# Half of the tokens take most of an input projection by Strassen's seven block products

## The chip, the cores and the metric

The kernel runs on one core of a Trainium2 chip. The core has five engines that each work through their own list of instructions in order: TensorE (PE, with a separate row PEld for its weight loads), VectorE (DVE), ScalarE (ACT), GpSimd (POOL) and SyncE (SP), which here only issues DMAs. An engine waits on semaphores for what the others produce. The metric is device time in microseconds (us) of one execution, as the median of several runs.

## The reference, cut to what matters

One layer over 2048 tokens of width 1024, in float32:

```python
h = _rmsnorm(x, norm_g[l])
proj = h @ w_in[l] + b_in[l]                       # 1024 -> 4096
ua, za, ub, zb, ga, gb = jnp.split(proj, SPLITS, axis=-1)
ya = _s5_branch(ua, ...) * jax.nn.silu(za)         # diagonal complex state-space scan, gelu, glu
yb = _pool_branch(ub, pool_w[l], pool_scale[l]) * jax.nn.silu(zb)   # causal means over 2, 4, 8, 16
merged = sigmoid(ga) * (ya @ w_branch_a[l]) + sigmoid(gb) * (yb @ w_branch_b[l])
x = x + merged @ w_out[l]
return _rmsnorm(x, final_norm_g)
```

The parts ua, za, ub and zb are 512 columns wide (4 tiles of 128 each, called UA, ZA, UB, ZB with a number), ga and gb 1024 (8 tiles each, GA and GB).

## The kernel before, in words

Tokens lie in four chunks of 512. Every product is done in three: each operand is cut into a high and a low part (`split`, L94: ACT writes the high part, DVE or POOL subtracts to get the low part), and `mm3` (L103 to L106) adds high*high, high*low and low*high in PSUM. A tile of 128 columns for one chunk is one block (`proj_block`, L594): 8 steps over the 1024 inputs, 24 matmuls of 128x512. The transposed, normalised input of a chunk, `hT`, is held in SBUF from its making to the end of the projection, all four chunks side by side.

The order of work is written out by hand; each engine does its share of it in the order of the text.

1. The ua part goes chunk by chunk. While a chunk's four blocks run, the next chunk is squared and summed on ACT (L544), scaled by POOL (L554), transposed on TensorE and cut (`transpose_tile`, L560). Chunk 3, say, is scaled beginning at the last block of chunk 1 and transposed behind the third block of chunk 2.
2. The za part: 4 tiles over 4 chunks, each block ending in `silu2` (L843: two passes of ACT from PSUM, one of DVE). After each block one step of the generator `matrices` is issued; its steps hold work on POOL (`outputs`, L477 to L479), DVE (`inputs`) and TensorE (L504, L507).
3. The ub and zb parts with the pooled means (`slide`, L877, L878 and L880; then L920) on DVE, cut by `cut_pooled`, multiplied on TensorE and scaled by `mix`. The cut of the means of one window is issued among the ub blocks of the next.
4. The ga and gb parts, 64 blocks. Each ends in one pass of ACT from PSUM (L1029) and a DMA. After each block one step of the generator `scan` is issued. A group u of it has 7 steps: `run_scan` (L749 to L766, all DVE), `table` (DVE), `run_taps` (TensorE), cuts, and last `run_out`, `run_in` and `gelu`, which run straight into the next `run_scan`: TensorE's small products (psy, psx), eight copies and a square on ACT, a pass of POOL (L784), two passes of DVE from PSUM (L787), a tanh, two more of DVE (L790). `phases` comes once, ahead of the first table.
5. The glu, branch and output products.

The projection's results lie in the PSUM pool `pmm`, four banks taken in turn (`mmtile`, L69); TensorE can begin a block only when the reader of the block four before it is done. Weights come from SP's DMAs one tile ahead (`pump`, L133).

## Time and profile before

| | us |
|---|---|
| median of 3 runs (lowest, highest) | 1214.21 (1213.85, 1217.29) |
| the profiled execution's own time | 1216.58 |
| its span | 1214.7 |
| TensorE busy | 1180.5 (97%) |
| VectorE busy | 731.5 (60%) |
| ScalarE busy | 395.0 (33%) |
| GpSimd busy | 345.9 (28%) |

The span is the time from the first to the last instruction that the profiler saw; the execution's own time is a little longer. Busy times of engines that are not awaited cost nothing. A matmul's row has a duration, but matmuls overlap: the distance between the starts of two of them is what one costs. TensorE's granted clock is given as a share of full speed: 1.00 is 2.4 GHz, and a stretch that reads less had some of its time at 1.2 GHz. In a timeline the number in brackets is the engine's idle time ahead of the instruction and who ended it.

### The profile page before, as it was taken

To read this page: it belongs to the slowest core of one execution; us is meant where nothing else is said; L and a number is where in the kernel's file an instruction comes from. 1 tells how busy PE (TensorE), PEld (TensorE's weight loads), DVE (VectorE), ACT (ScalarE), POOL (GpSimd) and SP (SyncE) were. 2 spreads that over 40 slices of the span, in tenths; PEclk is the share of its full clock that TensorE was granted. 3 is DMA by queue.
4 is the path that set the end of the run, shared out by engine and by line. 5 is a ranking of instruction groups with operands and counts; after the bars stand their busy time and mean duration, and the time that the engine had idled before them with its cause. 6 is when DMAs were issued, how large, how long until landed. Compare 5 with 4: busy or idle time off the path is not lost. (4 is left out here: it accounts for less than half of the span.)

```text
span 1214.7 us, 14777 instructions
## 1 busy us (share of the span) xinstructions
PE 1180.5 (97%) x5413; PEld 976.0 (80%) x5413; DVE 731.5 (60%) x1310; ACT 395.0 (33%) x622; POOL 345.9 (28%) x232
## 2 busy tenths in 40 slices
PE   7999989999999999999999999998999999999996
PEld 5887867888888888888888888886888888888885
DVE  5586389153543668777798773045665855755715
ACT  6542212222222232443333432244333332322302
POOL 3321077111111222422334321223562312213312
PEclk9999999999999999999999999999999999999998
DMA  8412334201111232433334332177766564563503
GB/s 297 139 44 77 67 108 135 81 18 55 44 46 44 86 111 88 132 96 109 113 95 131 98 101 81 69 233 241 255 217 224 172 196 136 182 212 109 191 1 104
DMA packets 149783, 149.94 MB, mean 123 GB/s; under 512 B 23584, under 2 KB 111184, under 8 KB 149712
## 3 DMA queue, kind: packets, MB, share of 16 engines
q1 hardware_dynamic: 127424, 112.28, 30.7%
q10 hardware_dynamic: 22288, 36.73, 8.0%
q8 instruction: 42, 0.69, 0.2%
q14 instruction: 29, 0.24, 0.1%
HBM read 99.43 MB, written 49.55 MB: 123 GB/s over the span
## 5 line engine op out<-in xcount | busy, mean ns | idle before, releaser
L104 PE MATMUL mm<-hT,wt 128*128 128x512 f32 x960 | 377.2, 393 | 0.0
L105 PE MATMUL mm<-hT,wt 128*128 128x512 f32 x960 | 375.6, 391 | 0.2 <-DVE hT L100 0.2
L106 PE MATMUL mm<-hT,wt 128*128 128x512 f32 x960 | 374.9, 390 | 0.0
L105 PEld LDWEIGHTS mm<-hT,wt 128*128 128x128 f32 x960 | 181.1, 189 | 38.0 <-DVE hT L100 1.3
L106 PEld LDWEIGHTS mm<-hT,wt 128*128 128x128 f32 x960 | 180.9, 188 | 38.0
L104 PEld LDWEIGHTS mm<-hT,wt 128*128 128x128 f32 x960 | 181.3, 189 | 36.8
L98 POOL TENSOR_TENSOR wt<-raw,wt 128x1024 fp32r<-128x1024 f32 x30 | 85.9, 2862 | 306.9 <-ACT wt L96 306.9
L1029 ACT ACTIVATE go<-mm,half 128x512 f32<-128x512 f32 x64 | 43.9, 687 | 192.5 <-PE mm L106 192.1
L104 PE MATMUL mm<-yab,wt 128*128 128x512 f32 x256 | 99.9, 390 | 0.1
L105 PE MATMUL mm<-yab,wt 128*128 128x512 f32 x256 | 99.7, 389 | 0.0
L106 PE MATMUL mm<-yab,wt 128*128 128x512 f32 x256 | 99.7, 389 | 0.0
L96 ACT ACTIVATE wt<-raw 128x1024 fp32r<-128x1024 f32 x62 | 65.5, 1057 | 57.2 <-PE mm L106 29.3
L1123 POOL TENSOR_TENSOR r<-r,gb 128x512 f32<-128x512 f32 (+1 forms) x33 | 40.9, 1257 | 135.3 <-ACT xt L1120 135.3
L1165 POOL TENSOR_TENSOR m<-gt 128x512 f32<-128x512 f32 x32 | 52.2, 1630 | 95.7 <-DVE gt L1163 64.5
L98 DVE TENSOR_TENSOR wt<-raw,wt 128x1024 fp32r<-128x1024 f32 x32 | 59.9, 1871 | 18.1 <-ACT wt L96 18.0
L847 ACT ACTIVATE st<-mm,half 128x512 f32<-128x512 f32 x32 | 22.0, 688 | 141.0 <-PE mm L106 104.8
L1163 DVE SCALAR_TENSOR_TENSOR gt<-gt,mm 128x512 f32<-128x512 f32 x64 | 42.3, 680 | 28.8 <-PE mm L106 24.3
L104 PEld LDWEIGHTS mm<-yab,wt 128*128 128x128 f32 x256 | 48.1, 188 | 10.9 <-issue 0.5
L106 PEld LDWEIGHTS mm<-yab,wt 128*128 128x128 f32 x256 | 48.1, 188 | 10.0
L105 PEld LDWEIGHTS mm<-yab,wt 128*128 128x128 f32 x256 | 48.1, 188 | 9.8
L105 PE MATMUL mm<-wo,mt 128*128 128x512 f32 (+1 forms) x136 | 51.2, 377 | 0.0
L106 PE MATMUL mm<-wo,mt 128*128 128x512 f32 (+1 forms) x136 | 51.2, 377 | 0.0
(272 smaller groups left out, 1918.2 us busy)
## 6 DMA issues: line engine op xcount, KB each, us to landing
xt<-in_x SPq DMA_DIRECT2D x32, 512.0 KB, 4.8
raw<-in_w_in SPq DMA_DIRECT2D x32, 512.0 KB, 4.2
Gd<-go ACTq DMA_DIRECT2D x64, 256.0 KB, 2.2
gt<-Gd SPq DMA_DIRECT2D x32, 512.0 KB, 4.9
raw<-in_w_branch_a SPq DMA_DIRECT2D x32, 256.0 KB, 2.8
raw<-in_w_branch_b SPq DMA_DIRECT2D x32, 256.0 KB, 3.2
out<-r ACTq DMA_DIRECT2D x32, 256.0 KB, 2.3
Ud<-uo ACTq DMA_DIRECT2D x16, 256.0 KB, 2.1
```

The source lines that it names most:

```text
L96: A.activation(hi, src, AF.Copy, scale=1.0 if scale is None else scale)
L98: (eng or V).tensor_tensor(out=lo, in0=src, in1=hi.bitcast(F32), op=ALU.subtract)
L104: PE.matmul(ps, lhsT=sh, rhs=mh, start=first, stop=False)
L105: PE.matmul(ps, lhsT=sh, rhs=ml, start=False, stop=False)
L106: PE.matmul(ps, lhsT=sl, rhs=mh, start=False, stop=last)
L847: A.activation(t, ps, AF.Tanh, bias=hcol(n), scale=0.5)
L1029: A.activation(o, ps, AF.Tanh, bias=hcol(n), scale=0.5)
L1123: GP.tensor_tensor(out=r, in0=r, in1=gb[:, cs], op=ALU.mult)
L1163: V.scalar_tensor_tensor(out=gt[:, b], in0=gt[:, b], scalar=1.0, in1=pss[b], op0=ALU.add, op1=ALU.mult)
L1165: GP.tensor_tensor(out=m, in0=gt[:, 0], in1=gt[:, 1], op=ALU.add)
```

## The change

The chunks are taken in the order 2, 3, 0, 1 (`CH`). For chunks 0 and 1 everything but the ua part is computed by Strassen's method in Winograd's form: a pair of column tiles, two chunks and two halves of the 1024 inputs make a 2x2 block product, and seven products of half-length blocks take the place of eight. There are 14 pairs. One run of seven is a `unit`.

- Seven slots of SBUF (`SLOTS`) hold the input's blocks B11, B21, B22 and their sums T1 to T4. `sums` and `last_sum` make them in the ua part of chunks 0 and 1. Chunks 2 and 3 use the same slots first; their transposed input is written to DRAM (`Hd`) and read back (`back`) in the last unit.
- `s_make` makes a pair's seven weight operands, among them four sums, three products ahead. Weight tiles other than ua's are loaded twice, 60 loads in place of 32; the pools `raw` and `w` have 3 buffers in place of 2.
- `unit` runs the seven products of 12 matmuls each. The first result is copied out of PSUM by ACT; the others are added by DVE (`plus`), and `sink` does what the tile's kind asks for. Results of ub and zb go by way of DRAM (`UBd`, `ZBd`).
- `matrices` is stepped in units 1 to 5, at every second product (`beside(0.5)`); `scan`, now with 6 steps a group, from unit 6 on at 0.36 of a step per product, then at 1.0 per za block, 0.4 per block of the ub, zb and ga parts, and 1.0 per gb block.
- Chunks 2 and 3 follow with ordinary blocks: za, then for each window two ub blocks, two zb blocks and four ga blocks, with the cuts and `mix` of that window's means among the ga blocks; then gb.

```diff
@@ -46,8 +46,8 @@
-    rawp = ctx.enter_context(tc.tile_pool(name="raw", bufs=2))
-    wp = ctx.enter_context(tc.tile_pool(name="w", bufs=2))
+    rawp = ctx.enter_context(tc.tile_pool(name="raw", bufs=3))
+    wp = ctx.enter_context(tc.tile_pool(name="w", bufs=3))
@@ -62,6 +62,9 @@
+    UBd = [dram.tile([128, 2, 512], F32, name=f"UBd{n}") for n in range(NB)]
+    ZBd = [dram.tile([128, 2, 512], F32, name=f"ZBd{n}") for n in range(NB)]
+    Hd = {c: [dram.tile([128, 2, 512], F32R, name=f"Hd{c}_{k}") for k in range(NK)] for c in (2, 3)}
...
@@ -172,14 +172,17 @@
+    CH = (2, 3, 0, 1)
+    SLOTS = ("B11", "T2", "B21", "T1", "T3", "B22", "T4")
+    s_slot = {name: ExitStack() for name in SLOTS}
+    slot = {name: sub(s_slot[name], "p" + name, "right").tile([128, 2, NB, 512], F32R, name=name) for name in SLOTS}
+    blocks = {2: ("T2", "T4"), 3: ("T3", "B22"), 0: ("B11", "B21"), 1: ("T3", "B22")}
+
+    def part(c, p, k):
+        return slot[blocks[c][k // NB]][:, p, k % NB, :]
...
@@ -561,42 +556,173 @@
+    def first_blocks(k):
+
+        wholes[k] = t = rawp.tile([128, 1024], F32, tag="raw", name="b11")
+        whole(t[:, 0:512], "B11", k, GP)
+        whole(t[:, 512:1024], "B21", k, GP)
+
+    def sums(k):
+
+        ps = [transpose_tile(1, k), transpose_tile(1, k + NB)]
+        t = wholes.pop(k)
+        t1, t4 = t[:, 0:512], t[:, 512:1024]
+        t2 = stg.tile([128, 512], F32, tag="stg", name="t2")
+        V.scalar_tensor_tensor(out=t1, in0=ps[0], scalar=gcol(k), in1=t1, op0=ALU.mult, op1=ALU.subtract)
+        V.scalar_tensor_tensor(out=t2, in0=ps[1], scalar=gcol(k + NB), in1=t1, op0=ALU.mult, op1=ALU.subtract)
+        V.tensor_tensor(out=t4, in0=t4, in1=t2, op=ALU.subtract)
+        for name, v in (("T1", t1), ("T2", t2), ("T4", t4)):
+            split(v, slot[name][:, 0, k, :], slot[name][:, 1, k, :], eng=V if name == "T2" else GP)
+
+    def last_sum(k):
+
+        t, t3 = (stg.tile([128, 512], F32, tag="stg", name="b12") for _ in range(2))
+        whole(t, "T3", k, GP)
+        whole(t3, "B22", k, V)
+        V.tensor_tensor(out=t3, in0=t3, in1=t, op=ALU.subtract)
+        split(t3, slot["T3"][:, 0, k, :], slot["T3"][:, 1, k, :])
...
+    def s_make():
+
+        m = s_now["made"]
+        s_now["made"] = m + 1
+        u, i = divmod(m, 7)
+        if m % 2 == 0:
+            s_now["w"] = wp.tile([128, 2, 1024], F32R, tag="w", name="ws")
+        o = s_ops[m] = s_now["w"][:, m % 2].rearrange("p (s n) -> p s n", s=2)
+            v = a11
+        elif i == 1:
+            s1 = s_now["s1"] = g1.tile([128, 512], F32, tag="s1", name="s1")
+            v = s_now["s2"] = g1.tile([128, 512], F32, tag="s2", name="s2")
+            V.tensor_tensor(out=s1, in0=a21, in1=a22, op=ALU.add)
+            V.tensor_tensor(out=v, in0=s1, in1=a11, op=ALU.subtract)
+        elif i == 2:
+            v = a12
+        elif i == 3:
+            v = s_now["s1"]
+        elif i == 4:
...
+        split(v, o[:, 0], o[:, 1], eng=GP)
+        if i >= 5:
+            s_load()
+    def unit(u, sink, hook, after=None):
+
+        n1, n2 = pairs[u]
+        def plus(out, p, t):
+            V.tensor_tensor(out=out, in0=ps[p], in1=t, op=ALU.add)
+
+        for i, name in enumerate(("B11", "T2", "B21", "T1", "T3", "B22", "T4")):
+            m = 7 * u + i
+            while s_now["made"] < min(m + 4, NP):
+                s_make()
+            ps.append(mmtile())
+            w, b = s_ops.pop(m), slot[name]
+            for k in range(NB):
+                cs = slice(k * 128, (k + 1) * 128)
+                mm3(ps[i], w[:, 0, cs], w[:, 1, cs], b[:, 0, k, :], b[:, 1, k, :], k == 0, k == NB - 1)
+            if i == 0:
+                t1 = g1.tile([128, 512], F32, tag="t1", name="t1")
+                A.activation(t1, ps[0], AF.Copy)
+            elif i == 1:
+                t2 = g1.tile([128, 512], F32, tag="t2", name="t2")
+                plus(t2, 1, t1)
+            elif i == 2:
+                plus(t1, 2, t1)
+                sink(n1, 0, t1, t1)
+            elif i == 3:
+                t3 = stg.tile([128, 512], F32, tag="stg", name="c12")
+                plus(t3, 3, t2)
+            elif i == 4:
+                plus(t2, 4, t2)
+                t = stg.tile([128, 512], F32, tag="stg", name="c22")
+                plus(t, 3, t2)
+                sink(n2, 1, t, t)
+            elif i == 5:
+                plus(t3, 5, t3)
+                sink(n1, 1, t3, t3)
+            else:
+                plus(t2, 6, t2)
+                sink(n2, 0, t2, t2)
+            hook()
+            if after:
+                after(i)
 
@@ -626,35 +752,55 @@
...
+    for p, c in enumerate(CH):
...
+            if p < 2 and n == 1:
+                for k in range(NB):
+                    for j in (k, k + NB):
+                        GP.dma_start(out=Hd[c][j], in_=slot[blocks[c][j // NB]][:, :, j % NB, :])
...
+            if p == 2:
+                if n == 0:
+                    first_blocks(0)
+                    first_blocks(1)
+                sums(n)
+                if n < 2:
+                    first_blocks(n + 2)
+            if n == 3 and p < 2:
+                norm_tiles(p + 2)
...
+            pv.issue((0, 18, 8, 12)[p])
+            if (p, n) == (2, 3):
+                s_x.close()
+                g1 = sub(s_g, "g1", "right")
+                for _ in range(3):
+                    s_load()
+            if p == 3 and n < 2:
+                s_make()
+                s_make()
+    for k in range(NB):
+        last_sum(k)
@@ -808,12 +954,13 @@
             sp = run_scan(u, xs)
+            if u + 1 < NU:
+                load_u(u + 1)
...
@@ -842,30 +989,91 @@
+    def sink(n, c, ps, o):
+        if n >= GA:
+            gate(n, c, ps, o)
+        elif n >= ZB:
+            silu2(d2, n, ps, o)
+            A.dma_start(out=ZBd[n - ZB][:, c], in_=o)
+        elif n >= UB:
+            A.activation(o, ps, AF.Identity, bias=bcol(n))
+            A.dma_start(out=UBd[n - UB][:, c], in_=o)
+        else:
+            silu2(d2, n, ps, o)
+            A.dma_start(out=SZd[c][:, n - ZA], in_=o)
...
+    def beside(rate):
+
+        nonlocal bg
+        credit[0] += rate
+        while credit[0] >= 1.0:
+            credit[0] -= 1.0
+            if bg is not None:
+                try:
+                    next(bg)
+                except StopIteration:
+                    bg = None
...
+    def back(i):
+
+        if i < 4:
+            c, h, name = ((2, 0, "B11"), (2, 1, "T2"), (3, 0, "B21"), (3, 1, "T1"))[i]
+            for k in range(NB):
+                GP.dma_start(out=slot[name][:, :, k, :], in_=Hd[c][h * NB + k])
+        if i in (3, 5):
...
+    for u in range(len(pairs)):
+        if u == 1:
+            pv.issue(len(pv.todo))
+            bg = matrices(d2)
+        if u == 6:
+            while bg is not None:
+                beside(1.0)
+            s_d.close()
+            s_par.close()
+            d4 = sub(s_scan, "d4")
+            bg = scan(d4)
+        unit(u, sink, (lambda: pv.issue(12)) if u == 0 else (lambda: beside(0.5 if u < 6 else 0.36)),
+             back if u == len(pairs) - 1 else None)
...
+    blocks.update({2: ("B11", "T2"), 3: ("B21", "T1")})
...
@@ -886,25 +1094,27 @@
...
+    def gate_block(n, c):
+        gate(n, c, proj_block(n, c), stg.tile([128, 512], F32, tag="stg", name="go"))
...
+        szs = [d3.tile([128, 512], F32, tag=f"szb{c}", name="szb") for c in range(NCH)]
+        SP.dma_start(out=ub[:, 0:4, 1:], in_=UBd[i].rearrange("p c (j k) -> p (c j) k", j=2))
+        for c in (0, 1):
+            SP.dma_start(out=szs[c], in_=ZBd[i][:, c])
+        for c in (2, 3):
...
+            beside(0.4)
...
+        for c in (2, 3):
+            silu2(d3, ZB + i, proj_block(ZB + i, c), szs[c])
+            beside(0.4)
         pump()
-        before = (i, pw, szs, pl)
+        for j in range(4):
+            n = GA + 6 - 2 * i + j // 2
+            cut_pooled(pl, j)
+            gate_block(n, 2 + j % 2)
+            mix(i, pw, szs[j], j)
+            beside(0.4)
+            if j % 2:
+                pump()
@@ -1015,32 +1221,24 @@
...
+    for i in range(NK):
+        last = i == NK - 1
+        for c in ((3, 2) if last else (2, 3)):
+            gate_block(GB + i, c)
+            beside(1.0)
```

The order on VectorE, first place: the gate part before, where the scan's group 1 runs (L790 is the last pass of gelu, L749 to L766 are `run_scan`; psy is the scan's PSUM).

```order
L790 SCALAR_TENSOR_TENSOR yo<-z,psy 128x512 x2
L749 TENSOR_TENSOR rot<-xs,tab 128x1024
L750 TENSOR_TENSOR xs<-xs,tab 128x1024
L751 TENSOR_TENSOR rot<-rot,xs 128x512
L752 TENSOR_TENSOR rot<-rot,xs 128x512
L756 SCALAR_TENSOR_TENSOR xs<-RD,rot 128x256 x4
L758 TENSOR_TENSOR rot<-xs,tab 128x1024
L759 TENSOR_TENSOR xs<-xs,tab 128x1024
L761 MEMSET sp 128x4
L766 TENSOR_TENSOR sp<-rot,xs 64x2x255 x4
L739 TENSOR_TENSOR tmp<-tab,UB 128x4 x2
```

The same stretch in the changed kernel, in unit 10: c_3472 and t_3425 are sums of that unit, mm a product in PSUM.

```order
L936 SCALAR_TENSOR_TENSOR yo<-z,psy 128x512 x2
L895 TENSOR_TENSOR rot<-xs,tab 128x1024
L896 TENSOR_TENSOR xs<-xs,tab 128x1024
L897 TENSOR_TENSOR rot<-rot,xs 128x512
L898 TENSOR_TENSOR rot<-rot,xs 128x512
L902 SCALAR_TENSOR_TENSOR xs<-RD,rot 128x256 x4
L904 TENSOR_TENSOR rot<-xs,tab 128x1024
L905 TENSOR_TENSOR xs<-xs,tab 128x1024
L907 MEMSET sp 128x4
L912 TENSOR_TENSOR sp<-rot,xs 64x2x255 x4
L689 TENSOR_TENSOR t_3425<-mm,t_3425 128x512
L689 TENSOR_TENSOR c_3581<-mm,t_3425 128x512
```

Before, no instruction of DVE around the group reads a projection block from PSUM; now the sum of the fourth product stands ahead of the group and those of the fifth behind it.

The order on VectorE, second place: the pooled means of window 16 before; szb are zb's results, plhl the cut means that TensorE waits for, psp their product.

```order
L925 TENSOR_TENSOR sa<-sb,rcnt 128x8
L926 TENSOR_TENSOR sa<-sa,ub 128x8
L925 TENSOR_TENSOR sa<-sb,rcnt 128x7
L926 TENSOR_TENSOR sa<-sa,ub 128x7
L849 SCALAR_TENSOR_TENSOR szb<-st,sz 128x512 x4
L98 TENSOR_TENSOR plhl<-sa,plhl 128x512
L894 SCALAR_TENSOR_TENSOR po<-psp,cols,szb 128x512
L98 TENSOR_TENSOR plhl<-sa,plhl 128x512
```

And now:

```order
L936 SCALAR_TENSOR_TENSOR yo<-z,psy 128x512 x2
L895 TENSOR_TENSOR rot<-xs,tab 128x1024
L896 TENSOR_TENSOR xs<-xs,tab 128x1024
L897 TENSOR_TENSOR rot<-rot,xs 128x512
L898 TENSOR_TENSOR rot<-rot,xs 128x512
L902 SCALAR_TENSOR_TENSOR xs<-RD,rot 128x256 x4
L904 TENSOR_TENSOR rot<-xs,tab 128x1024
L905 TENSOR_TENSOR xs<-xs,tab 128x1024
L907 MEMSET sp 128x4
L912 TENSOR_TENSOR sp<-rot,xs 64x2x255 x4
L101 TENSOR_TENSOR plhl<-sa,plhl 128x512
L1101 SCALAR_TENSOR_TENSOR szb<-psp,cols,szb 128x512
```

A whole group of the scan (gelu 3, `run_scan` 4) now stands between zb's results and the first cut of the means.

## Rows read from the trace of the kernel before

**Rows 1.** The page's head: span, and per engine busy time, share, instructions.

```profile
span 1214.7 us, 14777 instructions
PE 1180.5 (97%) x5413; PEld 976.0 (80%) x5413; DVE 731.5 (60%) x1310; ACT 395.0 (33%) x622; POOL 345.9 (28%) x232
```

**Rows 2.** Timeline of TensorE, za part: start, duration, engine, line, instruction.

```profile
129.05 0.39 PE L104 MATMUL mm<-hT,wt 128*128 128x512 f32 x1
...
131.09 0.39 PE L104 MATMUL mm<-hT,wt 128*128 128x512 f32 x1
```

**Rows 3.** Timeline of the ua part: TensorE's transposes, next block, POOL's scaling.

```profile
69.03 1.91 PE L563 MATMUL psT<-idn,xt 128*128 128x128 f32 x16
70.69 0.48 PE L104 MATMUL mm<-hT,wt 128*128 128x512 f32 x1
...
79.14 7.53 POOL L554 TENSOR_TENSOR xt<-xt,rsy 128x1024 f32<-128x1024 f32 x4 [18.30 <-DVE t L290]
```

**Rows 4.** Part with matrices: windows (span, busy per engine, clock, DMA), then timeline.

```profile
150.00:170.00 20.00, 14.72 (x74) 11.38 (x72) 18.07 (x17) 3.80 (x6) 18.65 (x11) 1.00 0.33 106
170.00:180.00 10.00, 9.78 (x43) 7.86 (x44) 6.22 (x10) 1.26 (x2) 2.90 (x2) 0.83 0.26 85
190.00:200.00 10.00, 9.38 (x49) 7.16 (x48) 9.90 (x10) 1.46 (x3) 9.23 (x6) 1.00 0.43 141
...
114.22 2.39 POOL L98 TENSOR_TENSOR wt<-raw,wt 128x1024 fp32r<-128x1024 f32 x1 [2.96 <-ACT wt L96]
142.31 1.22 POOL L477 TENSOR_TENSOR ca<-C,AR 128x576 f32<-128x576 f32 x1 [25.70 <-DVE C L448]
156.34 2.73 DVE L220 TENSOR_TENSOR bp<-bp,tmp 128x512 f32<-128x512 f32 x1
184.89 1.05 PE L504 MATMUL psk<-ca,B 128*16 128x128 f32 x8
```

**Rows 5.** Timeline of the gate part with scan: DVE, ACT and TensorE.

```profile
450.23 0.28 PE L104 MATMUL psx<-uu,bt 128*128 128x256 f32 x1
454.67 1.23 DVE L749 TENSOR_TENSOR rot<-xs,tab 128x1024 f32<-128x1024 f32 x1 [7.23 <-ACT xs L704]
463.51 2.78 DVE L766 TENSOR_TENSOR sp<-rot,xs 64x510 f32<-64x510 f32 x4
...
485.99 0.69 ACT L1029 ACTIVATE go<-mm,half 128x512 f32<-128x512 f32 x1 [1.36 <-PE mm L106]
495.43 1.22 DVE L749 TENSOR_TENSOR rot<-xs,tab 128x1024 f32<-128x1024 f32 x1
510.61 2.78 DVE L766 TENSOR_TENSOR sp<-rot,xs 64x510 f32<-64x510 f32 x4
...
525.51 0.28 PE L104 MATMUL psx<-uu,bt 128*128 128x256 f32 x1
526.95 0.40 PE L104 MATMUL mm<-hT,wt 128*128 128x512 f32 x1
```

**Rows 6.** Timeline of DVE: first and last instruction of phases, then of one table.

```profile
419.58 2.76 DVE L215 TENSOR_SCALAR phw<-PH 128x16 f32<-128x16 f32 x16
...
435.47 0.29 DVE L247 TENSOR_TENSOR UB<-UB,phw 128x128 f32<-128x128 f32 x1
...
551.57 0.24 DVE L739 TENSOR_TENSOR tmp<-tab,UB 128x4 f32<-128x4 f32 x2
...
558.50 0.42 DVE L742 TENSOR_TENSOR tab<-tmp 128x256 f32<-128x256 f32 x1
```

**Rows 7.** Timeline of DVE, window 16: first and last pass, then a cut.

```profile
254.40 2.03 DVE L877 TENSOR_TENSOR sa<-ub 128x1792 f32<-128x1792 f32 x1 [20.43 <-ACT ub L904]
...
266.26 2.29 DVE L920 SCALAR_TENSOR_TENSOR sa<-sb,ub 128x2048 f32<-128x2048 f32 x1
...
282.24 0.68 DVE L98 TENSOR_TENSOR plhl<-sa,plhl 128x512 fp32r<-128x512 f32 x1
```

**Rows 8.** Windows, the first 30 us: the last column is GB/s.

```profile
0.00:30.00 30.00, 20.99 (x99) 17.14 (x100) 15.35 (x35) 19.65 (x30) 9.77 (x30) 1.00 0.85 297
```

More of the change, by code (lines that the diff above doesn't have):

```diff
@@ L151, in load_next @@
         state["loaded"] = j + 1
-    w6 = None
     def plain(key):
-        pool = w6 if key[0] == "br" and (NK * key[1] + key[2]) % 3 == 2 else wp
-        t = pool.tile([128, 2, 1024], F32R, tag="w", name="wt")
+        t = wp.tile([128, 2, 1024], F32R, tag="w", name="wt")
         hl[key] = t
@@ L172, in branch_job @@
         add_job(("br", c, n), load, plain)
-    s_hT = [ExitStack() for _ in range(NCH)]
-    hT = [None] * NCH
-    def open_hT(c):
-        hT[c] = sub(s_hT[c], f"hTp{c}", "right").tile([128, 2, NK, 512], F32R, name=f"hT{c}")
-    for c in range(NCH - 1):
-        open_hT(c)
+    CH = (2, 3, 0, 1)
[5 more added lines that the diff above has]
+        return slot[blocks[c][k // NB]][:, p, k % NB, :]
     s_x = ExitStack()
@@ L189, in hybrid_kernel @@
     d1 = sub(s_d, "d1")
-    firsts = {n: d1.tile([128, 2, 1024], F32R, name=f"w_first{n}") for n in (2, 3)}
+    firsts = {n: d1.tile([128, 2, 1024], F32R, name=f"w_first{n}") for n in (3,)}
     def w_first(key):
@@ new lines, in hybrid_kernel, with s_load @@
+    s_g = ExitStack()
+    pairs = [(UB + 3, UB + 2), (UB + 1, UB), (ZB + 3, ZB + 2), (ZB + 1, ZB), (ZA, ZA + 1), (ZA + 2, ZA + 3)]
+    pairs += [(GA + i, GA + i + 1) for i in range(0, NK, 2)] + [(GB + i, GB + i + 1) for i in range(0, NK, 2)]
+    NP = 7 * len(pairs)
+    s_raws, s_ops, s_now = {}, {}, {"loaded": 0, "made": 0}
+    def s_load():
+        m = s_now["loaded"]
+        s_now["loaded"] = m + 1
+        if m >= 2 * len(pairs):
+            load_next()
+            return
+        n = pairs[m // 2][m % 2]
+        raw = s_raws[m] = rawp.tile([128, 1024], F32, tag="raw", name="raw")
+        SP.dma_start(out=raw.rearrange("p (k n) -> p k n", k=NK),
+                     in_=w_in[0][:, n * 128:(n + 1) * 128].rearrange("(k p) n -> p k n", p=128))
@@ L825, in scan @@
                 bt = load_m(BTd[u + 1])
+            yield
+            yield
+            if u + 1 < NU:
                 cut_u(u + 1)
-                if u + 2 < NU:
-                    load_u(u + 2)
-            for _ in range(3):
-                yield
+            yield
             shl = two("sp", K, "spl")
@@ L843, in silu2 @@
     def silu2(d, n, ps, o):
[L845 removed]
         t = d.tile([128, 512], F32, tag="st", bufs=1, name="st")
         A.activation(t, ps, AF.Tanh, bias=hcol(n), scale=0.5)
[L848 to L853 removed]
+        A.activation(o, ps, AF.Identity, bias=bcol(n))
+        V.scalar_tensor_tensor(out=o, in0=t, scalar=1.0, in1=o, op0=ALU.add, op1=ALU.mult)
@@ new lines, in hybrid_kernel @@
+    credit = [0.0]
+    bg = None
[8 more added lines that the diff above has]
+                except StopIteration:
+                    bg = None
+    half1 = [ZA + i for i in range(NB)]
+    for i in reversed(range(NB)):
+        half1 += [UB + i, ZB + i, GA + 6 - 2 * i, GA + 7 - 2 * i]
+    for n in half1 + [GB + i for i in range(NK)]:
+        w_in_job(n, plain)
@@ L854, in hybrid_kernel @@
+    s_g.close()
+    for name in ("T4", "B22", "T3"):
+        s_slot[name].close()
+    blocks.update({2: ("B11", "T2"), 3: ("B21", "T1")})
+    d3 = sub(s_d, "d3")
     for i in range(NB):
-        for c in range(NCH):
+        for c in (2, 3):
             ps = proj_block(ZA + i, c)
             o = stg.tile([128, 512], F32, tag="stg", name="zo")
-            silu2(d2, ZA + i, ps, o)
+            silu2(d3, ZA + i, ps, o)
             A.dma_start(out=SZd[c][:, i], in_=o)
-            next(bg, None)
+            beside(1.0)
@@ L861, in hybrid_kernel @@
         pump()
-    for _ in bg:
-        pass
-    s_d.close()
-    s_par.close()
-    d3 = sub(s_d, "d3")
     ub = d3.tile([128, T, K + 1], F32, name="ub")
@@ L905, in hybrid_kernel @@
                          bias=bcol(UB + i))
-            if before:
-                mix(*before[:3], c)
+            beside(0.4)
         pwr = d3.tile([128, 128], F32, tag="pwr", name="pwr")
@@ L994, in hybrid_kernel @@
             branch_job(c, n)
-    d4 = sub(s_d, "d4")
-    bg = scan(d4)
     d5 = e5 = None
```

180 lines of the change are left out of this document (79 added, 101 removed).

## The prediction

> **What bounds the kernel now.** The page's head comes first: TensorE is busy 1180.5 of 1214.7 us [rows 1]. So a matmul that is left out is worth its full time, and every wait of TensorE that appears costs its full time; what counts of the other engines is when they release TensorE. The sum is made against the profiled execution's own time, 1216.6, which is 2.4 above the median.
>
> What a matmul costs is read from TensorE's timeline by distances: nine of 128x512 start in 131.09 - 129.05 = 2.04 us, 0.2267 each [rows 2]. A block of 24 is then 5.44 us, a Strassen product of 12 is 2.72. The windows of the part with `matrices` come next, for they hold the one long stop of before: from 150 to 170 us TensorE works 14.72 of 20 us, beside DVE's 18.07 and POOL's 18.65, and in the 10 us behind it the granted clock is 0.83, some of it at 1.2 GHz in place of 2.4 [rows 4]. DVE and POOL are thus near their limit where they work together. Last the scan's timeline: what DVE does at one stretch there [rows 5].
>
> **What is removed.** A pair of tiles for two chunks took 4 blocks, 96 matmuls; seven products take 84. 14 pairs save 168 matmuls: 168 x 0.2267 = -38.1 us.
>
> **What is added, in the order of the run.**
>
> *The ua part of chunk 1.* `sums(0)` stands behind the first block of chunk 0's turn, where before three blocks stood ahead of the transposes of the last chunk. Its transposes need all four tiles that POOL scales. Before, the block began at 70.69 and the scaling ended at 79.14 + 7.53 = 86.67 [rows 3]; a block later TensorE is at 76.13 and stands for 10.5 us. If DVE's part of the scaling's chain, which ended 18.30 us of POOL's waiting [rows 3], comes forward by some 3 us for having fewer parameter instructions ahead, it is 7.5. I take +10.5. Writing `Hd` lies beside these blocks: 0.
>
> *`matrices` beside units 1 to 5.* One of its steps comes per two products, 5.44 us, where it came per block of 5.44: the same pace. New beside it are two weight operands per step, 128x512 each: 2.39 us for 128x1024 without neighbours [rows 4], so 2.4 a step on POOL, and a difference now and then, less the weight tile that POOL cut before: about 2.5 per step. Eight of the steps fill POOL; 8 x 2.5 = 20, less the three products that the operands are ahead (8.2): 12 at most, 0 at least. I take 8, as POOL has little room in that stretch, and subtract the stop that stands there already, 20 - 14.72 = 5.3 [rows 4]: about +3 (-5.3 to +6.7).
>
> *`scan` beside units 6 to 13.* This decides. In units DVE is on TensorE's path: each product but the first is read out of its bank by `plus`, in the order of DVE's list, and there are four banks. TensorE can so run four products, 10.88 us, past an instruction of DVE, then it waits. Before, ACT read the gate blocks' banks, and what DVE did was no matter. The scan's work now comes in bursts between two sums (the order shows one). Of a burst I need its length and what TensorE still has to do:
> - `phases`: 419.58 to 435.76, 16.2 us [rows 6], and a sum of 0.7; less 10.88: 6. With POOL's work beside it up to 11. I take +9.
> - `run_scan` alone: 454.67 to 466.29, 11.6 us; with POOL beside it 495.43 to 513.39, 18.0 [rows 5]. In a unit POOL can be at most three operands ahead (3 x 1.2 us and a difference of 1.2) before it too stands still; so I take 13, nearer to 11.6, and keep both ends.
> - ahead of groups 1 to 7 the gelu runs straight into `run_scan`. From the end of the block, when ACT's pass begins, to the first pass of `run_scan` it is 495.43 - 485.99 = 9.44 us [rows 5]; DVE's own passes stand in there in order, so its list is closed for all of it. TensorE has its small products meanwhile: twelve in 526.95 - 525.51 = 1.44 [rows 5], twice that for `run_out` and `run_in`, 2.88.
> - group 0 (unit 8, product 1): from psx to the scan 454.67 - 450.23 = 4.44 [rows 5]; 4.44 + 13 + 0.69 for the sum - 1.44 - 10.88 = 5.8 (4.4 to 10.8).
> - group 1 (unit 10, product 3): the fourth result is needed again with the fifth, so only three products are free, 8.16: 9.44 + 13 + 1.38 - 2.88 - 8.16 = 12.8 (11.4 to 17.8).
> - group 2 (unit 12, product 6): the next product is copied out by ACT, so five are free: 9.44 + 13 + 0.69 - 2.88 - 13.6 = 6.7 (5.3 to 11.6).
> - group 3 falls among za blocks, ACT's to read, with the next DVE need far off: 0. A table takes 558.92 - 551.57 = 7.35 [rows 6], under 10.88: 0 in the units.
>
> Together 9 + 5.8 + 12.8 + 6.7 = +34.
>
> *`scan` among the ub, zb and ga blocks.* Here DVE is awaited for the cut means (plhl) and `mix`. The means of window 16 take 268.55 - 254.40 = 14.15 us [rows 7]; the two zb blocks behind them last 10.88, and the gelu chain takes 9.44 more, so the means hold nothing up by themselves. But group 4 now stands ahead of the first cut of window 16, as the order's second place shows. From the end of the last zb block DVE needs 9.44 + 13 + 0.68 for the cut, TensorE has one ga block (5.44) and the small products (2.88): it stands for 14.8 (13.4 to 19.8). Group 5 stands ahead of `mix` in window 4: 9.44 + 13 + 0.69 + 0.68 - 2.88 - 10.88 = 10 (8.6 to 15). Two tables between two `mix`: 7.35 and 1.4 of cut and `mix` less a block's 5.44, 3.3 each, +6.6 (0 to 6.6). Groups 6 and 7 fall among gb blocks, which ACT reads: 0. Together +31.5.
>
> *The read-back.* 8.39 MB in the last unit's first four products. The best stretch shown moves 297 GB/s [rows 8]: 28 us, with the last quarter wanted 24.5 us after the first issue: +4. None of before's DMAs is issued by POOL; if one costs POOL nothing it is 0, if it costs as much as its own 576-column pass, 1.22 us [rows 4], four per product and the operand's cut are 7.3 against 2.72, at most 4 x 4.6 = 18. I take +4 (0 to 20). SP's raw loads, 28 more, are ahead by three products each: 0.
>
> *The clock.* After a long stop 10 us at 0.83 lose 1.7 us [rows 4]. Five such stops at most 8.5; I take +5 (0 to 8.5), as a stop can be short.
>
> **The sum.** -38.1 + 10.5 + 3 + 34 + 31.5 + 4 + 5 = +50; 1216.6 + 50 - 2.4 = 1264. With all low ends (7.5, -5.3, 27, 22, 0, 0) it is +13, 1227; with all high ends (10.5, 6.7, 51, 41, 20, 8.5) +100, 1314.
>
> A pass of DVE of 128x512 took 2.73 us beside POOL [rows 4], one of the same size elsewhere 0.68 [rows 7]: the two slow each other. The Trainium skill, page "SBUF — State Buffer", section "Who interferes with whom", says more: a DVE instruction with two SBUF inputs and a GpSimd instruction that reads SBUF exclude each other, and the second to issue "fully blocks" until the first ends. The trace agrees in kind; that busy times of 9.90 and 9.23 in the same 10 us [rows 4] hold waiting as work is how the rule would read them.
>
> **Rivals.**
> 1. *Slower still: DVE and POOL add up instead of running side by side.* By rows: per two products POOL has three passes of `outputs` (3 x 1.22 [rows 4]), two operands (2 x 1.2) and 4/7 of a difference (0.57 x 1.2), 6.7 us; DVE has three passes of `inputs` (3 x 0.68 [rows 7]) and about 1.2 of `s_make`'s sums and copies, 3.2. In turn that is 9.9 against TensorE's 6.5 with its small products (1.05 [rows 4]). Eight steps x 3.4 - 8.2 = 19 in place of 3: 1280. For it: the 2.73. Against: sums read PSUM, and before's stretch from 190 to 200 kept TensorE at 9.38 of 10 [rows 4]. This is what the Trainium skill's rule above would make of it.
> 2. *Faster: the bursts fit into the banks.* From the point where a burst and its gelu stay under some 14 us (10.88 and 2.88), the scan costs nothing: -38.1 + 10.5 + 3 + 4 = -20.6, and 1193. For it: TensorE works through everything before, at 97%. Against: 9.44 + 11.6, both measured, are already 21.
> 3. *Half of it:* gelu's chain is shorter behind a product than behind a gate block, as ACT and POOL have less queued, and stops let later ones find DVE ahead. Half of 34 + 31.5 + 5: -38.1 + 10.5 + 3 + 33 + 2 + 2 = +12.4, 1227.
> 4. *The read-back is late:* POOL's issue takes the 18 above: 1280. The Trainium skill, same page, section "Who interferes with whom", warns that POOL's own DMAs starve while DVE holds the port; no run here shows one.
>
> **Chances.** Main 0.6, rivals 0.1, 0.12, 0.12 and 0.06. Within 0.3% (3.6 us, about what a measurement of this kernel can tell from no change) gets 0.06, half of rival 3, which may end 10 us lower than worked out. Faster is rival 2, 0.12; slower is the rest, 0.82. The likeliest case's own range is 1227 to 1314. The range for 8 times in 10, 1219 to 1308, takes in rival 3 and leaves out rival 2 and the last of the high ends.
>
> **What would show it.** In the changed profile: TensorE's waits on DVE's `plus`, each behind an instruction of `run_scan`, in units 8, 10 and 12 and behind `phases`; a wait for plhl of some 15 us in window 16; a wait of the transposes for POOL's scaling near 76 us; a clock below 1.00 behind each; GB/s near 300 in the last unit. Each is a term with its size. It is wrong if TensorE stays above 97% busy in units 6 to 13: then DVE's list wasn't closed as long as I say, and the time is below 1214.

## The result and the profile after

The changed kernel takes 1405.9 us (four runs, 1402.8 to 1407.1) against 1215.7 before: ratio 1.156, interval 1.153 to 1.159. It is slower, as forecast, but by 190 us and not by 50; the time lies far above the range.

The page's head of the changed kernel, for [rows 1]:

```profile
span 1404.4 us, 15221 instructions
...
PE 1205.0 (86%) x5245; PEld 975.7 (69%) x5245; DVE 868.1 (62%) x1464; ACT 472.5 (34%) x750; POOL 554.3 (39%) x410
```

TensorE has 168 matmuls fewer, and yet its busy time has grown by 24.5 us. Its idle time has grown from 34.2 (1214.7 - 1180.5) to 199.4. Both want an explanation: the busy time should have fallen by 38.1, so 62.6 us are added to it, and 165.2 to the idle time.

Who ended TensorE's idle time in the changed kernel, by line: us in all, times, the longest one.

```profile
PE mm L107 <- ACT ws L99: 38.6, 8, 11.2
PE psp L108 <- DVE plhl L101: 32.9, 5, 12.9
PE mm L107 <- DVE t L689: 23.0, 4, 13.3
PE psk L501 <- POOL ca L476: 15.4, 6, 4.7
PE mm L107 <- ACT yhl L99: 10.9, 3, 6.5
PE mm L107 <- ACT wt L99: 8.3, 1, 8.3
```

The wait of the forecast, a bank that VectorE's sum (L689) has not yet read, is third. The first is the cut of a weight operand (ws) by ScalarE.

The place of [rows 5], now in unit 10 of the changed kernel, from the timelines of VectorE, ScalarE and TensorE; in brackets the idle time ahead and who ended it.

```profile
462.37 2.19 DVE L895 TENSOR_TENSOR rot<-xs,tab 128x1024 f32<-128x1024 f32 x1
...
472.17 2.78 DVE L912 TENSOR_TENSOR sp<-rot,xs 64x510 f32<-64x510 f32 x4
474.98 0.69 DVE L689 TENSOR_TENSOR t<-mm,t 128x512 f32<-128x512 f32 x1
...
476.43 0.72 ACT L999 ACTIVATE c<-c,half 128x512 f32<-128x512 f32 x1 [14.29 <-DVE c L689]
...
475.82 0.77 PE L107 MATMUL mm<-B,ws 128*128 128x512 f32 x1 [13.32 <-DVE t L689]
476.38 0.63 PE L108 MATMUL mm<-B,ws 128*128 128x512 f32 x1
476.81 0.63 PE L109 MATMUL mm<-B,ws 128*128 128x512 f32 x1
...
481.24 0.39 PE L108 MATMUL mm<-T,ws 128*128 128x512 f32 x1
481.46 0.39 PE L109 MATMUL mm<-T,ws 128*128 128x512 f32 x1
```

This stop was forecast at 12.8 us, and it is 13.3. Two things were not in the forecast. ScalarE stands for 14.29 us as well, behind a pass that waits for the sum, and the weight cuts are queued behind that pass. And behind the stop the matmuls start 0.43 us apart (476.81 - 476.38), against 0.23 five microseconds later (481.46 - 481.24): the granted clock has fallen to its lower level (it reads 0.50 from 467.3 to 480.9 us). [rows 2] has 0.2267.

The burst of `phases` in unit 6 shows the other kind of stop, as the timelines have it:

```profile
351.99 0.68 DVE L664 TENSOR_TENSOR s<-raw 128x512 f32<-128x512 f32 x1
352.76 0.69 DVE L665 TENSOR_TENSOR s<-s,raw 128x512 f32<-128x512 f32 x1
353.55 0.63 ACT L99 ACTIVATE ws<-s 128x512 fp32r<-128x512 f32 x1 [17.19 <-DVE s L665]
354.23 0.80 PE L107 MATMUL mm<-T,ws 128*128 128x512 f32 x1 [11.24 <-ACT ws L99]
```

The weight sums s1 and s2 of `s_make` are VectorE's too and stand behind the burst; ScalarE waits 17.19 us for them. No bank is short here: the weight operand is.

In the part with `matrices` the mean clock is 0.80 over 75 us (windows of the changed kernel; [rows 4] had 0.83 in one stretch of 10), with a stop for POOL's ca in six of the eight steps, such as these (timeline of TensorE):

```profile
225.00:300.00 75.00, 54.66 (x218) 41.83 (x219) 57.45 (x63) 18.61 (x29) 51.38 (x35) 0.80 0.32 102
```

```profile
229.20 1.89 PE L501 MATMUL psk<-ca,B 128*16 128x128 f32 x8 [4.68 <-POOL ca L476]
233.18 1.08 PE L504 MATMUL psb<-idn,bp 128*128 128x128 f32 x4 [2.09 <-DVE bp L217]
```

### The profile page after: what moved, and what is told of

The parts are those of the page before. It is cut to its first block, busy times and chain, and to the rows that moved or that the text cites. A ratio compares the mean times of both kernels' runs of the same rounds, so it can differ in the third digit from the quotient of the medians.

```text
span 1404.4 us, 15221 instructions
## 1 busy us (share of the span) xinstructions
PE 1205.0 (86%) x5245; PEld 975.7 (69%) x5245; DVE 868.1 (62%) x1464; ACT 472.5 (34%) x750; POOL 554.3 (39%) x410
## 5 line engine op out<-in xcount | busy, mean ns | idle before, releaser
L107 PE MATMUL mm<-T,ws 128*128 128x512 f32 x224 | 95.4, 426 | 37.2 <-ACT ws L99 37.2
L107 PE MATMUL mm<-B,wt 128*128 128x512 f32 x272 | 112.4, 413 | 14.3 <-ACT wt L99 8.3
L108 PE MATMUL mm<-B,wt 128*128 128x512 f32 x272 | 111.7, 411 | 0.6 <-DVE B L103 0.6
L109 PE MATMUL mm<-B,wt 128*128 128x512 f32 x272 | 110.8, 407 | 1.5 <-POOL wt L101 1.5
L107 PE MATMUL mm<-T,wt 128*128 128x512 f32 x272 | 108.2, 398 | 4.2 <-ACT T L99 4.2
L108 PE MATMUL mm<-T,wt 128*128 128x512 f32 x272 | 107.3, 395 | 2.7 <-DVE T L103 2.7
L109 PE MATMUL mm<-T,wt 128*128 128x512 f32 x272 | 106.7, 392 | 0.0
L101 POOL TENSOR_TENSOR ws<-s,ws 128x512 fp32r<-128x512 f32 x42 | 55.6, 1324 | 115.1 <-ACT ws L99 115.1
L109 PE MATMUL mm<-T,ws 128*128 128x512 f32 x224 | 94.0, 420 | 4.5 <-POOL ws L101 3.8
L101 POOL TENSOR_TENSOR ws<-raw,ws 128x512 fp32r<-128x512 f32 x56 | 74.2, 1332 | 54.8 <-ACT ws L99 54.8
L108 PE MATMUL mm<-T,ws 128*128 128x512 f32 x224 | 92.9, 415 | 0.0
L107 PE MATMUL mm<-B,ws 128*128 128x512 f32 x168 | 71.0, 422 | 24.5 <-DVE t L689 23.0
L107 PEld LDWEIGHTS mm<-T,ws 128*128 128x128 f32 x224 | 46.1, 206 | 49.7 <-ACT ws L99 41.0
L107 PEld LDWEIGHTS mm<-B,wt 128*128 128x128 f32 x272 | 54.5, 200 | 26.7 <-ACT wt L99 8.7
L109 PE MATMUL mm<-B,ws 128*128 128x512 f32 x168 | 69.3, 413 | 1.9 <-POOL ws L101 1.7
```

The lines of the kernel that those rows point to most:

```text
L101: (eng or V).tensor_tensor(out=lo, in0=src, in1=hi.bitcast(F32), op=ALU.subtract)
L107: PE.matmul(ps, lhsT=sh, rhs=mh, start=first, stop=False)
L108: PE.matmul(ps, lhsT=sh, rhs=ml, start=False, stop=False)
L109: PE.matmul(ps, lhsT=sl, rhs=mh, start=False, stop=last)
```

## The experiments

### Where the scan lies

e1 takes the scan out of the units, at a whole step per block in the three places of the window stage.

```diff
-        unit(u, sink, (lambda: pv.issue(12)) if u == 0 else (lambda: beside(0.5 if u < 6 else 0.36)),
+        unit(u, sink, (lambda: pv.issue(12)) if u == 0 else (lambda: beside(0.5 if u < 6 else 0.0)),
...
-            beside(0.4)
+            beside(1.0)
```

> Edit: no step of the scan beside units 6 to 13; all of it from the za blocks of chunks 2 and 3 on, one step per block. Theory A (the scan's bursts close VectorE's list to the units' sums and to the weight sums): units 6 to 13 run at 7 x 2.72 = 19.05 us each, TensorE's idle time there (61 us in the changed kernel) falls under 8, and about 15 us of low clock go with it; some 30 come back in the stage of the pooled means, where more groups now fall. Time about 1355. Theory B (the units themselves, their weight operands on POOL and ACT and their sums, can't keep TensorE's pace): units 6 to 13 stay above 22 us each and the time above 1390.

Measured 1421.6 us (ratio 1.168, 1.164 to 1.171). The two halves of theory A part here. The units come out as it says, in e1's windows:

```profile
320.00:505.00 185.00, 176.30 (x765) 142.42 (x764) 60.04 (x112) 68.70 (x107) 109.46 (x93) 1.00 0.49 154
```

ScalarE's copies of the first products stand 16.2, 18.9 and then five times 19.0 us apart in units 6 to 13, and the clock is 1.00. So units without the scan keep TensorE's pace; theory B falls. But far more than 30 us come back: the same steps now close the lists around the means, with stops up to this one in e1's timeline:

```profile
768.60 0.80 PE L107 MATMUL psp<-plhl,pw 128*128 128x512 f32 x1 [22.68 <-ACT plhl L99]
```

The scan hid before since nothing in the 64 gate blocks awaited VectorE. In the changed order only the gb blocks at the end are left of such a stretch, so moving the scan moves the stops.

### Matrices at a lower density

The scan starts behind the last unit, as in e1.

```diff
-        unit(u, sink, (lambda: pv.issue(12)) if u == 0 else (lambda: beside(0.5 if u < 6 else 0.0)),
+        unit(u, sink, (lambda: pv.issue(12)) if u == 0 else (lambda: beside(0.17)),
```

> Edit: as e1_scan_after_units, and the steps of matrices are spread over units 1 to 13 at 0.17 per product in place of 0.5 in units 1 to 5. Theory A2 (density: POOL has 6.7 us of work per step against 5.44 of TensorE, and falls behind): the stops for ca and bp, 22 us of idle time in the changed kernel, nearly go, and 8 us of low clock with them: 30 us less than e1. Theory B2 (POOL and VectorE exclude each other, so the same work costs the same wherever it lies): less than 10 us below e1.

Measured 1409.3, 12 below e1: between the two. The waits for ca and bp are gone, and the distance from the first unit's first copy to the last's falls from 299 to 284 us, against 254 without matrices (e14 below). Density is part of it, with 12 of the 30 us that A2 expected; the rest stays, partly as waits for POOL's weight cuts (13.4 us against 3.0 in e1, 7.8 of it in one stop).

### The sums out, and SyncE's queue

e3 leaves out the additions of the seven products: ScalarE copies each one. The two weight sums of VectorE go to POOL.

```diff
-            V.tensor_tensor(out=s1, in0=a21, in1=a22, op=ALU.add)
-            V.tensor_tensor(out=v, in0=s1, in1=a11, op=ALU.subtract)
+            GP.tensor_tensor(out=s1, in0=a21, in1=a22, op=ALU.add)
+            GP.tensor_tensor(out=v, in0=s1, in1=a11, op=ALU.subtract)
...
-            V.tensor_tensor(out=out, in0=ps[p], in1=t, op=ALU.add)
+            A.activation(out, ps[p], AF.Copy)
```

> Edit: the changed kernel, but each product is copied out of PSUM by ScalarE without the sum, and the two weight sums of VectorE are made by POOL; this leaves out the additions of Strassen's results. The scan lies where it did. Theory A: with VectorE off the units' path the stops of units 6 to 13 (61 us idle, some 17 of clock) fall by three quarters, time about 1345. Theory B: they stay, as POOL has even more to do: time 1400 or above.

Measured 1404.7: nothing gained, so theory A fails as it was put: VectorE is off the units' path, and TensorE stands as long. Theory B does not follow either, since e1 shows clean units. The timelines of POOL and SyncE in e3 name a third thing:

```profile
412.68 1.26 POOL L664 TENSOR_TENSOR s<-raw 128x512 f32<-128x512 f32 x1 [21.62 <-DMA raw<-in_w_in]
...
399.55 3.62 SPq L826 DMA_DIRECT2D U<-Ud  x8
403.26 4.78 SPq L828 DMA_DIRECT2D mzr<-Kd  x8
408.15 1.16 SPq L646 DMA_DIRECT2D raw<-in_w_in  x2
```

`load_u` now shares its buffer with what `run_scan` reads, so SyncE's list waits for the last pass of `run_scan`, then needs 8.6 us to issue 16 DMAs; only then come the raw weights. Three runs put `load_u` two steps later, e5 in the changed kernel, e6 in e3, e7 in e1:

```diff
             sp = run_scan(u, xs)
-            if u + 1 < NU:
-                load_u(u + 1)
             yield
...
             run_taps(u)
+            if u + 1 < NU:
+                load_u(u + 1)
```

> Edit: the changed kernel with load_u two steps later, behind run_taps. Theory S (SyncE's queue is closed too: load_u takes the buffer that run_scan still reads, SyncE waits for its last pass, 88 us in all in the changed kernel, then needs 9 us to issue 16 DMAs, and the raw weights and the pool matrices stand behind it): the stops that end with a late raw load go, 3.6 in unit 9 and 8.3 and 1.5 in the za part, and some of the 7.5 ahead of a mix; about 20 us idle and 6 of low clock, time about 1380. Rival (VectorE and ScalarE are closed in the same stretches anyway): less than 8 us.

> Edit: as e3_sums_left_out (no sums behind the products, the weight sums on POOL), and load_u two steps later. Theory S: of e3's 70 us of waits for weights cut by ScalarE the 45 in units 6 to 13 were raw weights held up on SyncE's queue; they go, and 10 us of low clock: time about 1350. Rival (ScalarE is held by its own waits for the scan): within 10 us of e3's 1405.

> Edit: as e1_scan_after_units, and load_u two steps later. Theory S: the waits of the means' products for their cut on ScalarE (46 us, behind pool matrices and the ub rows that came 27.7 and 7.8 us late) fall to a third, those on VectorE (51 us) stay: time about 1385 against e1's 1421. Rival (the scan is a chain that needs some 50 us a group wherever it lies): within 10 us of 1421.

Measured: e5 1409.1 (the rival is right, no gain), e6 1381.5 (23 below e3; theory S had 55), e7 1412.1 (10 below e1; S had 36, its rival up to 10). SyncE's queue is a cause only where the sums don't stand beside the scan. In the changed kernel three lists are closed in the same stretches, VectorE's, ScalarE's and SyncE's, and to open VectorE's (e3) or SyncE's (e5) alone gains nothing; ScalarE's was not opened alone.

### Length of a step, lookahead of the weights

e4 puts a `yield` behind the gelu and inside `run_scan`, `table` and `phases`, and raises the rates 2.24 times; e15 makes the operands one product earlier, as below; e16 is e4 with both e15's and e5's edit.

```diff
-            while s_now["made"] < min(m + 4, NP):
+            while s_now["made"] < min(m + 5, NP):
```

> Edit: the changed kernel with the scan's steps cut finer: run_scan in four pieces behind the gelu, a table in three, phases in four, and 2.24 times the steps per block or product, so that the scan goes on at the same pace. Theory A, length of a burst decides: no burst is longer than the four products that the banks cover, stops in units 6 to 13 fall to under 15 us and those in the pooled stage by half: time about 1330. Theory C, the amount decides: per product VectorE has some 1.0 us of sums and, at this pace, 0.06 x 40 = 2.4 us of scan against 2.72 of TensorE, so TensorE still loses some 0.7 us per product, 39 us in units 6 to 13: time about 1380.

> Edit: the changed kernel with the weight operands made four products ahead in place of three. Theory W (in a burst the three operands, 8.2 us, run out before the four banks, 10.9): the 39 us of waits for ScalarE's weight cuts in 8 stops become shorter by up to 2.7 us each, 15 to 20 us, the low clock stays as there are as many stops: time about 1388. Theory P (the banks run out at the same time, and each closed list only hands over to the next): less than 6 us.

> Edit: as e4_fine_steps, with the operands four products ahead and load_u two steps later. Theory W: the waits for weights of e4 (20.6 and 14.3 us, 30 short ones) fall by two thirds, time about 1370. Theory P: within 8 us of e4's 1394.

Measured 1393.9, 1394.6 and 1398.2. With fine steps no stop in the units is above 7.1 us, but there are more of them and units 6 to 12 take 27 to 35 us each: from the first unit's first copy to the last's it is 378 us, as in the changed kernel, so the 12 us are gained behind the units. Theory A, the length of a burst, fails. Theory C, the amount of VectorE's work at this pace, comes nearer, though at 1394 even C was too low; and it isn't shown to be the amount alone, for VectorE is busy 163 of the 209 us from 325 to 534, and TensorE's waits there end with weight cuts more often than with sums. In e15 waits for ws became waits for the sums (12.1 and 10.8 us at the places where ws took 11.2 and 10.1): operands and banks run out almost together, and 11 us are gained, between W and P. e16 gains nothing over e4, as theory P has it.

### What a stop costs beside its length

In the kernel before, behind the pass of each gate block (b is 0 in the ga part, 1 in the gb part):

```diff
+            if c % 2 and not last:
+                for r in range(6 * b):
+                    A.activation(o, o, AF.Copy)
+                pe = mstile("pst")
+                PE.matmul(pe[:, 0:128], lhsT=o[:, 0:128], rhs=o[:, 0:128], start=True, stop=True)
```

> Edit: the kernel before, with a small matmul behind every second block of the gate part that reads the block's result: TensorE stands for one pass of ScalarE (about 1 us, 16 times in the ga part) and for seven (about 4.5 us, 14 times in the gb part; the copies are in place and change nothing). Theory K, a stop costs its length and about 1.5 to 2 us of matmuls at the low clock, a short one as much as a long one: idle 80, low clock 30 x 1.75 = 52, time about 1350. Rival, the clock's price goes with the length (1.7 us for 5.3 in the kernel before): idle 80, low clock 25, time about 1320; and the ga part shows a clock above 0.97.

Measured 1332.9. e8's windows of the ga and of the gb part, and two stops of its timeline:

```profile
425.00:600.00 175.00, 164.88 (x788) 135.58 (x787) 121.63 (x241) 58.71 (x97) 46.81 (x26) 1.00 0.33 100
647.50:895.00 247.50, 185.83 (x773) 153.54 (x772) 83.18 (x137) 102.58 (x165) 33.86 (x21) 0.88 0.19 59
```

```profile
647.12 0.80 PE L1034 MATMUL pst<-go 128*128 128x128 f32 x2 [4.74 <-ACT go L1032]
...
648.14 0.63 PE L105 MATMUL mm<-hT,wt 128*128 128x512 f32 x1
648.57 0.63 PE L106 MATMUL mm<-hT,wt 128*128 128x512 f32 x1
...
652.27 0.39 PE L104 MATMUL mm<-hT,wt 128*128 128x512 f32 x1
652.50 0.39 PE L105 MATMUL mm<-hT,wt 128*128 128x512 f32 x1
```

```profile
665.34 0.80 PE L1034 MATMUL pst<-go 128*128 128x128 f32 x2 [4.74 <-ACT go L1032]
...
666.36 0.41 PE L106 MATMUL psy<-spl,ca 128*128 128x256 f32 x1
666.57 0.41 PE L104 MATMUL psy<-spl,ca 128*128 128x256 f32 x1
```

Short stops, 0.78 us each and 10 us in the first window, leave the clock at 1.00: theory K is wrong for them. Each of the 14 long ones (4.74) is followed by matmuls at the lower level. Behind seven of them seven to thirteen of 128x512 start 0.43 apart in place of 0.23, as in the first stop shown; behind the other seven it is a dozen of the scan's small products, 0.21 apart in place of 0.12, as in the second. That is 1.3 to 2.7 us a stop, 1.7 on average and 24 in all, which is what the rival had for the low clock (25). All long stops of e8 have one length, so it can't tell whether the price goes with the length, as the rival says. The changed kernel can: behind its 13.3 us stop above there are twelve slow matmuls, behind one of 2.6 us (at 542.92, clock 0.50) ten, and behind one of 1.4 us (at 517.73, clock 1.00) none at that distance. So the price goes with the number of stops that bring the lower level, hardly with their length; of stops near 2 us some bring it and some don't.

### The parts left out one after the other

Both kernels without the scan, then without `matrices` too. In e9 and e11 the zeros written in the scan's place held raw weights up on SyncE's queue (units 6 to 9 took 20 to 27 us); e13 and e14 write them with four DMAs, as below. The second edit is that of e11, e12 and e14.

```diff
     def scan(d):
+        zero = d.tile([128, 2048], F32, name="zero")
+        GP.memset(zero, 0.0)
+        for n in range(NB):
+            SP.dma_start(out=Yd[n].rearrange("t g c k -> (t g c k)").rearrange("(p f) -> p f", p=128), in_=zero)
+            yield
...
-            bg = matrices(d2)
+            bg = iter(())
```

> Edit: the changed kernel with the whole scan left out (its results are written as zeros). Theory D (the scan's share decides; units, means and sums are clean without it): left are the ua part (19 us over before), the last sums and parameters in units 0 and 1 (11), matrices (27 with its clock), the read-back and the glu stage (10), against 38 of matmuls saved: some 30 above the kernel before without its scan, about 1211. Rival (units and means stall by themselves): 80 or more above it.

> Edit: the kernel before with the whole scan left out in the same way. All theories: it hid but for its small products on TensorE, 8 x 3 x 1.44 = 35 us, so about 1181.

> Edit: as e9_after_no_scan, and matrices left out as well. Theory D: the 27 us of matrices and 17 of its products go: about 1163 to 1168, within 10 us of the kernel before without both, as the 38 saved are spent on the ua part, units 0 and 1 and the read-back. Rival (POOL's weight operands and sums hold the units by themselves): 1200 or more.

> Edit: the kernel before without scan and without matrices. All theories: matrices' small products (17 us) and its one long stop (5 and 2 of clock) go as well: about 1157.

> Edit: the changed kernel with the scan left out, its results written as zeros by four DMAs. Theory (the zeros' 64 DMAs cost e9 some 15 us): about 1231, 53 above e10; the scan's share of the +190 is then 137. Rival (no matter): within 4 us of e9's 1246.

> Edit: the same without matrices as well. Theory: about 1186, 28 above e12; units 6 to 13 run at 19.0 us as in e1, units 2 to 5, whose results ScalarE and VectorE pass through silu, stay at 21.4. Rival: within 4 us of e11's 1201.

Measured: e9 1246.4, e10 1178.2, e11 1201.4, e12 1158.4, e13 1231.2, e14 1184.7. The last two meet their theory within 2 us, so e9 and e11 carried 15 to 17 us of their own making. By e13 and e14 the scan's share is large, but neither theory of e9 and e11 holds: the changed kernel stays 53 and 26 us above the kernel before without the same parts, where theory D had 30 and under 10, and the rivals 80 in e9 and a time of 1200 at least in e11. e10 and e12 keep the many small writes of zeros; no wait of TensorE for a weight shows in either. Heads of e13, e14, e10 and e12, in this order:

```profile
span 1230.9 us, 13566 instructions
...
PE 1138.2 (92%) x4957; PEld 924.8 (75%) x4957; DVE 629.7 (51%) x976; ACT 403.0 (33%) x614; POOL 495.4 (40%) x368
```

```profile
span 1182.8 us, 13171 instructions
...
PE 1117.2 (94%) x4853; PEld 908.0 (77%) x4853; DVE 566.6 (48%) x902; ACT 403.2 (34%) x614; POOL 454.6 (38%) x344
```

```profile
PE 1142.3 (97%) x5125; PEld 940.1 (80%) x5125; DVE 483.4 (41%) x822; ACT 323.9 (28%) x486; POOL 282.5 (24%) x190
```

```profile
PE 1126.9 (98%) x5021; PEld 929.7 (81%) x5021; DVE 422.6 (37%) x748; ACT 323.6 (28%) x486; POOL 242.8 (21%) x166
```

The spans of e10 and e12 are 1174.9 and 1153.3 us. Subtracting heads (after less before, then part by part) gives TensorE's idle time and its busy time above the matmuls of each part:

| part | idle, forecast | idle, measured | busy above the matmuls, measured |
|---|---|---|---|
| scan | 65.5 | 105.1 | 28.6 |
| matrices | 3 | 20.9 | 5.6 |
| all else (forecast: ua 10.5, read-back 4) | 14.5 | 39.2 | 28.4 |
| sum | 83 | 165.2 | 62.6 (forecast 5, all clock) |

With -38.1 for the matmuls that is 189.7, the difference of the spans. The scan's share is measured with `matrices` present, that of `matrices` with the scan gone; taken out in another order they could come out otherwise.

## Why the prediction was wrong

Right were the sign, the -38.1 (5413 to 5245 matmuls), the place of the scan's stops and the size of those that a full list of banks explains. Forecast and found: group 1 12.8 and 13.3, group 2 6.7 and 6.8, and, without banks, window 4 10 and 10.9, the ua part's transposes 10.5 and 7.7. `phases`, 9 and 11.2, came near by luck, and group 0, 5.8 and 10.1, did not: both ended with a weight cut and not with a bank. In window 16 TensorE stands 7.5 and, one matmul later, 12.9, together 20.4 against 14.8; "the means hold nothing up by themselves" failed there, as ScalarE stood 10.59 us for a zb result behind them.

**The step that failed by most is "The clock": "Five such stops at most 8.5; I take +5".** A stop's price was about right: 1.7, against 1.7 on average in e8 and some 1.3 in the changed kernel (52 us over 39 stops). Their number was wrong: the changed kernel has 39 stops of over 1.2 us (174 us in all), five in the kernel before. The sum itself has seven of over 5 us and gave a clock to five; it gave none to the stops that it had not priced. By the distances of its matmuls of 128x512 (those over 0.26, against 0.2267) 52 us are lost, 47 of them in stretches of the lower granted clock; in the kernel before it is 7 and 4. Of the 62.6 that leaves 17: 7 in small products and 10 in the last matmul ahead of each stop, which shows its whole 0.39 us. The Trainium skill, page "TensorE: Matmul & The Clock Gate", section "What's actually happening", calls the penalty of the warm-up less than 1% of a typical kernel span. It speaks of one warm-up; with a ramp behind most of 39 stops it is 52 of 1404 here, and the measurement decides.

**The second is "TensorE can so run four products, 10.88 us, past an instruction of DVE".** It took the banks for the only thing that runs out. ScalarE's list closes with VectorE's (14.29 and 17.19 us above), and SyncE's too (POOL's 21.62 in e3), weight operands are only 8.2 us ahead, and 39 us of waits end with a weight cut. e1 shows that the scan is the cause of the units' stops, e3 that VectorE's sums alone aren't, e6 and e15 that each reserve hands over to the next. TensorE's idle time was forecast at 83 us and is 165.

**The third are the terms set at 0.** Their places in the changed kernel, from the timelines of ScalarE and TensorE:

```profile
621.35 0.33 ACTq L1074 DMA_DIRECT2D SZd<-zo  x1
629.59 0.63 ACT L99 ACTIVATE ca<-mr 128x512 fp32r<-128x512 f32 x1 [6.54 <-DVE zo L995]
...
121.50 0.80 PE L107 MATMUL mm<-T,wt 128*128 128x512 f32 x1 [4.18 <-ACT T L99]
159.69 0.79 PE L107 MATMUL mm<-T,ws 128*128 128x512 f32 x1 [6.59 <-ACT ws L99]
631.22 0.80 PE L107 MATMUL mm<-B,wt 128*128 128x512 f32 x1 [8.30 <-ACT wt L99]
673.29 0.80 PE L107 MATMUL psp<-plhl,pw 128*128 128x512 f32 x1 [7.53 <-ACT plhl L99]
...
570.67 0.76 PE L107 MATMUL mm<-B,wt 128*128 128x512 f32 x1 [5.96 <-issue]
```

- "group 3 falls among za blocks, ACT's to read ...: 0": a za block's result passes through VectorE and back to ScalarE's queue, whose DMA waits for it: 8.3 us.
- "Groups 6 and 7 ...: 0": the glu stage waits 10.9 us for cuts of the scan's results, 3.0 in the kernel before.
- Units by themselves cost more than 0: the ua part's last chunk waits 4.18 for a cut of its input, unit 0 waits 6.59 for a weight cut, with the last sums ahead of it, and units 2 to 5, whose results go through `silu2`, take 21.4 to 22.9 us each in e14 in place of 19.05. That ScalarE comes to the weight cuts late there is a reading of the order, not a run of its own.
- "A table takes ... under 10.88: 0 in the units": in unit 13 a table took 12.6 us (556.5 to 569.1), 4.2 of it in one pass held up beside POOL (last section), and TensorE stood 5.96. The profile names no releaser, but the matmul begins with the first sums behind the table. In e15 the same table took 9.3 us, and the stop behind it is 2.35.
- `matrices`: +3 was 21 idle. I let the weight lookahead of 8.2 us absorb POOL's surplus; TensorE's small products wait for POOL's ca in six of the eight steps, and no lookahead of another operand helps them.

**The rivals.** Rival 1 (POOL and VectorE take turns) named a place, `matrices`, at 19 us against 3, and 21 came; whether it is the exclusion or plain amount isn't settled by e2. Rivals 2 and 3 (the bursts fit, or half of them) fell with the first rows. Rival 4's price was too high: POOL issues four read-backs in 2.95 us, not 4.9, and e14, which issues the same, shows stops of under 3 us in that unit.

The 28 us of busy time in "all else" are, by e12 and e14, 20 in the distances of the matmuls of 128x512 (16 of it in stretches of the lower clock), 7 in the last matmul ahead of a stop and 2 in transposes. What stays open is how much of e3's loss is ScalarE's, and what ScalarE's list would give if it alone were opened. e14 bears on the practical question: with no scan and no matrices at all the changed kernel is still 26 us slower than the kernel before without them. Unless their own products on TensorE happen to fill its stops, no place for them in this order makes it faster. No complete version tried beats the kernel before.

## What to carry to other kernels

Saving matmuls on an engine that is 97% busy pays only if the engines that feed it keep pace in every stretch; ask of each instruction that now stands on the path what its engine does in the 20 us ahead of it, on all of the in-order lists and the DMA queue. Count the stops, long or not, and price the low clock by their number: here it took some 1.3 us for each of over 1.2 us, 1.7 behind those of 4.74, and nothing behind those of 0.78. Where background work was hidden by a stretch that did not await its engine, look for that stretch in the new order first: if it is gone, moving the work moves the stops.
